# A hybrid encoder step on one core: the last two turns of the down projection as plain block products, the output stored in two parts, and the last h pair split inside its operand tiles

## The chip, the core and the metric

The kernel runs on one core of a Trainium2 chip. The time is that of one execution on the device, in microseconds (us); of several runs the median counts. The engines are TensorE (PE, with its weight loads shown as PEld), VectorE (DVE), ScalarE (ACT), GpSimd (POOL) and SyncE (SP), which here only issues DMAs. Each engine runs its own instructions in order and waits on semaphores for the others; ACT and POOL issue DMAs of their own as well.

## The reference, cut to what matters

One layer on 512 prompt frames (with 16 meta tokens ahead of them) and 64 sample frames: RMSNorm, a joint input projection, a pooling mixer and a differential attention, an output projection, and then the part that the change touches, a SwiGLU block and the last RMSNorm:

```python
D_MODEL, D_FF = 2048, 5632

def _rmsnorm(x, g, eps=EPS):
    xf = x.astype(jnp.float32)
    y = xf * lax.rsqrt(jnp.mean(xf * xf, axis=-1, keepdims=True) + eps)
    return (y * g.astype(jnp.float32)).astype(x.dtype)

def _swiglu(h, g_ffn, w_gate, w_up, w_down):
    n = _rmsnorm(h, g_ffn)
    return h + (jax.nn.silu(n @ w_gate) * (n @ w_up)) @ w_down

    y_prompt = _rmsnorm(h_p[:, N_META:], g_final)
    y_sample = _rmsnorm(h_s, g_final)
```

Everything is float32. The 512 + 64 = 576 tokens behind the block are handled together; the outputs are 512 and 64 rows of 2048.

## The kernel before

**Number format.** Each float32 operand of a product is split into a high part (a copy into TensorE's reduced format, on ACT) and a low part (the difference, on DVE). A product is three matmuls: high x high, high x low, low x high (L808 to L810). Tokens lie in the free dimension, in two halves of TN = 288.

**Seven products for eight.** The class `Seven` multiplies a weight block (2 x 2 blocks of 128) with an operand (2 feature rows x 2 token halves) by a scheme of seven block products. `prep` forms the sums and differences of weight blocks on DVE (L793 to L797) and splits the seven weight operands; `product` runs their matmuls for all feature pairs of the turn; `evac` adds the results in PSUM to the output.

**The down projection.** Its operand h, 5632 features by 576 tokens, is held in DRAM as 22 feature pairs `hd[0]` to `hd[21]`, each already combined into the seven operands of the scheme. In the numbering of these operands, index 0 is feature row 0 with token half 0, 3 is row 1 with half 0, 5 is row 1 with half 1, and 2 is the difference of the two halves of row 0. Pairs 0 to 20 are stored split (high and low); pair 21, the last made, is stored unsplit. A pair comes into SBUF as three tiles of two operands (`hc`, q = 0, 1, 2) and one half tile (`hh`, q = 3).

The work is 40 turns: five rounds over eight row pairs m of the output (256 output features each), each turn with up to five h pairs. The staggered `starts` give turns 32 to 39, the last round, 5, 5, 4, 4, 3, 3, 2 and 2 h pairs. A full turn is 7 x 5 x 3 = 105 matmuls, one of the last two 7 x 2 x 3 = 42. Turns alternate between the PSUM pools `mm` and `pj`. Row pair m of the output is added up in SBUF as `yt[m]`, four blocks of 288 tokens. Some of the sums go by an accumulating DMA from POOL: the shared first product in round 3 (L1106) and, for m under 6, two pieces of the last round by way of the buffers `ev` (L1101, L1102).

**Order.** The program is written in the order of the products, with `prep` three products ahead; `hooks` runs after each product. It loads an h pair when its first use is at most two turns off and a tile is free, behind the weight loads of the next turn on SP's queue. Pair 21 is read in seven pieces through two `ev` buffers, each then split into its `hc` tile by ACT (L1005) and DVE (L1006).

**The end.** `rows_out(m)` turns row pair m back into token rows: transposes on PE by 128 x 128 (L1136), the sum of squares on ACT (L1139), the product with the gain on DVE (L1142, L1146) into `yo`. It runs in the turn after the one that finishes the row pair. There are five token tiles (0 to 3 of 128 rows, 4 of 64). After the last row pair all five get their scale 1/rms at once (L1175 to L1182), and then `yo` is scaled and stored in 18 pieces of 256 KB (L1190 to L1194).

Of the kernel before, what the change touches and what calls it, by code (L numbers as in the profile page):

```python
# [50 lines left out]
def hymba_step(  # L51
# [945 lines left out]
    def h_operand(f, q):  # L997
        w, t = 2 if q < 3 else 1, h_slot(f, q)
        if f < NFP - 1:
            nc.sync.dma_start(out=t.bitcast(F32), in_=hd[f][:, 2 * q:2 * q + w])  # L1000
            return
        for i in range(w):
            s = dw.tile([P, TN], F32, name="ev", tag="ev", bufs=2)
            nc.sync.dma_start(out=s, in_=hd[f][:, 2 * q + i, 0])
            nc.scalar.activation(t[:, i, 0], s, AF.Copy)  # L1005
# [110 lines left out]
    def rows_out(m):  # L1116
# [5 lines left out]
        if m % 2 == 0:  # L1122
            for t in (0, 2):
                yo[t, m // 2] = full_slot([P, 1152], "yo", dtype=F32)[:, :1024].rearrange("p (t c) -> p t c", t=2)
        if m % 4 == 0:
            yo[4, m // 4] = full_slot([P, 1152], "yo", dtype=F32)[:, :1024]
        st, c0 = stat, m * 2 * P
        g = gfin[m // 4][:, c0 % 1024:c0 % 1024 + 256]
        for t in (0, 2, 4):
            nt = 2 if t < 4 else 1  # L1130
            rows = TT[t][1]
            pt = pz.tile([P, 512], F32, name="mm", tag="mm").rearrange("p (t c) -> p t c", t=2)[:rows, :nt]
            for u in range(nt):
                for i in range(2):
                    t0 = TT[t + u][0]
                    nc.tensor.transpose(out=pt[:, u, i * P:i * P + P], in_=hrow(2 * m + i)[:, t0:t0 + rows], identity=ident)  # L1136
            for u in range(nt):
                jk = dw.tile([P, 256], F32, name="jk", tag="jk", bufs=2)[:rows]
                nc.scalar.activation(jk, pt[:, u], AF.Square, accum_out=st[:rows, t + u, m:m + 1])  # L1139
# [93 lines left out]
```

## Time and profile before

| | us |
|---|---|
| median of 3 runs | 2314.15 |
| lowest, highest | 2313.45, 2318.22 |
| the profiled execution | 2311.8 |
| its span | 2310.0 |
| TensorE busy in it | 2252.7 |
| turn 31 starts | 2177.48 |
| turn 38 starts | 2270.35 |
| last transposes start | 2287.81 |
| first store issued | 2293.09 |

The span is the time from the first to the last event of the profiled execution; the execution's own time is 1.8 us longer. A row of a timeline has the start, the duration, the engine, the line, the operation and the names of output and inputs; in brackets is the idle time of the engine ahead of it and what ended it. Matmuls overlap in a pipeline, so the pitch from start to start is what one costs, not its duration.

### The profile page before, as it was taken

The page shows a single profiled execution, that of the slowest core. Times are in us where ns is not written, and L with a number is a line of the kernel's source. Part 1 is how long each engine was busy: PE and PEld are TensorE (multiplying, and loading weights), DVE is VectorE, ACT ScalarE, POOL GpSimd, SP SyncE. Part 2 cuts the span into 40 slices and gives each one's busy share as a digit, 9 for nine tenths or more (in the row PEclk, how much of TensorE's full clock was granted, in tenths as well). Part 3 has the DMA queues.
Part 4 walks back from the last instruction along what each step waited for, and adds up shares of the span by engine and source line. Part 5 has one row for each costly group of instructions (what it writes and reads, how often), then busy time and mean ns, then how long its engine had stood idle before and what let it go on. Part 6 is the DMA issues. An engine that isn't in the chain of part 4 may idle for free.

```text
span 2310.0 us, 43435 instructions
## 1 busy us (share of the span) xinstructions
PE 2252.7 (98%) x16815; PEld 2230.6 (97%) x16815; DVE 1904.8 (82%) x3496; ACT 1113.4 (48%) x2305; POOL 499.9 (22%) x452
## 2 busy tenths in 40 slices
PE   7999999999999899999999999999999999999995
PEld 6999999999999899999999999999999999999995
DVE  6888888875477889998999999999897788888787
ACT  5666666643244544444444444444444533333354
POOL 1100001000234223333343343333333000000110
PEclk9999999999999999999999999999999999999998
DMA  6433333323324244454444444435446778766844
GB/s 171 115 93 97 97 89 102 86 66 92 85 65 139 81 139 143 128 154 146 136 137 154 137 135 150 149 122 159 150 128 226 226 221 222 212 200 187 225 98 117
DMA packets 427362, 322.28 MB, mean 140 GB/s; under 512 B 13107, under 2 KB 397421, under 8 KB 427156
## 3 DMA queue, kind: packets, MB, share of 16 engines
q1 hardware_dynamic: 403616, 248.17, 36.7%
q0 software_dynamic: 22704, 69.90, 11.0%
q8 instruction: 132, 2.16, 0.4%
q10 hardware_dynamic: 836, 1.43, 0.2%
q14 instruction: 74, 0.61, 0.1%
HBM read 255.33 MB, written 62.03 MB: 137 GB/s over the span
## 4 chain that ended last, share of the span: by engine, by line
PE 89%; issue 5%; DVE 3%; DMA 1%; POOL 1%; ACT 1%; SPq 0%; POOLq 0%; DVEq 0%; ACTq 0%
PE mm L808 10%; PE pj L808 10%; PE pj L810 10%; PE mm L810 10%; PE pj L809 10%; PE mm L809 10%; PE pj L112 6%; PE pj L114 6%; PE pj L113 6%; PE mm L114 3%; PE mm L112 3%; PE mm L113 3%; PE S L426 1%; PE S L425 1%; PE T L454 1%
## 5 line engine op out<-in xcount | busy, mean ns | idle before, releaser
L838 DVE TENSOR_TENSOR ws<-raw,ws 128x512 fp32r<-128x512 f32 x430 | 393.9, 951 | 57.1 <-ACT ws L837 56.9
L837 ACT ACTIVATE ws<-raw 128x512 fp32r<-128x512 f32 x430 | 264.0, 629 | 360.6 <-DVE raw L795 121.1
L808 PE MATMUL mm<-xc,ws 128*128 128x288 f32 x1232 | 365.4, 297 | 7.6 <-ACT ws L837 7.4
L808 PE MATMUL pj<-xc,ws 128*128 128x288 f32 x1232 | 365.1, 296 | 3.1 <-ACT ws L837 3.1
L809 PE MATMUL mm<-xc,ws 128*128 128x288 f32 x1232 | 363.4, 295 | 0.0
L809 PE MATMUL pj<-xc,ws 128*128 128x288 f32 x1232 | 363.2, 295 | 0.0
L810 PE MATMUL pj<-xc,ws 128*128 128x288 f32 x1232 | 361.8, 294 | 0.8 <-DVE ws L838 0.8
L810 PE MATMUL mm<-xc,ws 128*128 128x288 f32 x1232 | 361.7, 294 | 0.2 <-DVE ws L838 0.2
L112 PE MATMUL pj<-x,ws 128*128 128x296 f32 (+1 forms) x1024 | 317.9, 311 | 9.6 <-DMA lv<-in_lambda_q_dram 5.2
L113 PE MATMUL pj<-x,ws 128*128 128x296 f32 (+1 forms) x1024 | 307.2, 300 | 0.0
L114 PE MATMUL pj<-x,ws 128*128 128x296 f32 (+1 forms) x1024 | 305.7, 299 | 0.0
L808 PEld LDWEIGHTS mm<-xc,ws 128*128 128x128 f32 x1232 | 232.0, 188 | 8.4 <-ACT ws L837 8.0
L808 PEld LDWEIGHTS pj<-xc,ws 128*128 128x128 f32 x1232 | 232.0, 188 | 3.3 <-ACT ws L837 3.3
L810 PEld LDWEIGHTS pj<-xc,ws 128*128 128x128 f32 x1232 | 233.2, 189 | 1.1 <-DVE ws L838 1.1
L810 PEld LDWEIGHTS mm<-xc,ws 128*128 128x128 f32 x1232 | 233.3, 189 | 0.4 <-DVE ws L838 0.4
L809 PEld LDWEIGHTS mm<-xc,ws 128*128 128x128 f32 x1232 | 233.0, 189 | 0.1
L809 PEld LDWEIGHTS pj<-xc,ws 128*128 128x128 f32 x1232 | 232.9, 189 | 0.0
L137 ACT ACTIVATE ws<-wraw,vcols 128x128 fp32r<-128x128 f32 x512 | 169.4, 392 | 106.9 <-PE pj L114 87.9
L1082 ACT ACTIVATE ws<-raw 128x640 fp32r<-128x640 f32 (+3 forms) x190 | 130.5, 688 | 184.1 <-PE mm L810 68.4
L112 PEld LDWEIGHTS pj<-x,ws 128*128 128x128 f32 x1024 | 193.2, 189 | 14.7 <-ACT x L106 9.6
L113 PEld LDWEIGHTS pj<-x,ws 128*128 128x128 f32 x1024 | 194.2, 190 | 0.4
L114 PEld LDWEIGHTS pj<-x,ws 128*128 128x128 f32 x1024 | 193.1, 189 | 0.0
(369 smaller groups left out, 5738.3 us busy)
## 6 DMA issues: line engine op xcount, KB each, us to landing
raw<-in_w_up_dram SPq DMA_DIRECT2D x88, 512.0 KB, 3.8
raw<-in_w_gate_dram SPq DMA_DIRECT2D x84, 512.0 KB, 5.0
hc<-hd SPq DMA_DIRECT2D x63, 576.0 KB, 6.0
raw<-in_w_down_dram SPq DMA_DIRECT2D x112, 320.0 KB, 7.1
wraw<-in_w_in_dram SPq DMA_DIRECT2D x64, 512.0 KB, 4.1
wraw<-in_w_out_dram SPq DMA_DIRECT2D x32, 512.0 KB, 4.0
hd<-hi POOLq DMA_DIRECT2D x21, 576.0 KB, 3.5
hd<-ho POOLq DMA_DIRECT2D x21, 576.0 KB, 4.2
```

What stands on the lines that cost most here:

```text
L112: nc.tensor.matmul(ps, lhsT=w(0), rhs=x(0), start=first, stop=False)
L113: nc.tensor.matmul(ps, lhsT=w(0), rhs=x(1), start=False, stop=False)
L114: return nc.tensor.matmul(ps, lhsT=w(1), rhs=x(0), start=False, stop=last)
L137: nc.scalar.activation(ws[:, 0, k, :], r[:, k, :], AF.Copy, scale=g)
L425: nc.tensor.matmul(ps, lhsT=self.q[:, m, qs], rhs=kt[:, m, c0:c1], start=True, stop=False)
L426: nc.tensor.matmul(ps, lhsT=self.q[:, 2 + m, qs], rhs=kt[:, m, c0:c1], start=False, stop=True)
L808: nc.tensor.matmul(ps, lhsT=w(0), rhs=x(0), start=first and j == 0, stop=False, skip_group_check=True)
L809: nc.tensor.matmul(ps, lhsT=w(0), rhs=x(1), start=False, stop=False, skip_group_check=True)
L810: mm = nc.tensor.matmul(ps, lhsT=w(1), rhs=x(0), start=False, stop=j == self.nj - 1, skip_group_check=True)
L837: nc.scalar.activation(ws[:, 0], src[:, k:k + WK], AF.Copy)
L838: nc.vector.tensor_tensor(ws[:, 1], src[:, k:k + WK], ws.bitcast(F32)[:, 0], op=ALU.subtract)
L1082: nc.scalar.activation(ws[:, 0], src, AF.Copy)
```

## The change

The code shown here is the part that decides; the arithmetic of the scale is rearranged too (a reciprocal and four short DVE operations in place of a reciprocal and five), and `rows_out` takes a list of token tiles, of 128-column blocks and of the column for its sum of squares.

```diff
+    PLAIN = 2
...
         if f < NFP - 1:
             nc.sync.dma_start(out=t.bitcast(F32), in_=hd[f][:, 2 * q:2 * q + w])
             return
-        for i in range(w):
-            s = dw.tile([P, TN], F32, name="ev", tag="ev", bufs=2)
-            nc.sync.dma_start(out=s, in_=hd[f][:, 2 * q + i, 0])
-            nc.scalar.activation(t[:, i, 0], s, AF.Copy)
-            nc.vector.tensor_tensor(t[:, i, 1], s, t.bitcast(F32)[:, i, 0], op=ALU.subtract)
+        nc.sync.dma_start(out=t.bitcast(F32)[:, :, 1], in_=hd[f][:, 2 * q:2 * q + w, 0])
+        whole.append((7 * now[0][0] + now[0][1] + 4, t))
+
+    def h_split(t):
+        f = t.bitcast(F32)
+        tc.keep_in_program_order(nc.scalar.activation(t[:, :, 0], f[:, :, 1], AF.Copy))
+        tc.keep_in_program_order(nc.vector.tensor_tensor(t[:, :, 1], f[:, :, 1], f[:, :, 0], op=ALU.subtract))
...
-        if queue and i in (0, 2, 4, 6) and first_use[queue[0][0]] <= n + 2 and h_free(*queue[0], n, i):
+        if whole and whole[0][0] <= 7 * n + i:
+            h_split(whole.pop(0)[1])
+        if queue and i in (0, 2, 4, 6) and first_use[queue[0][0]] <= n + 2 + queue[0][0] // 20 and h_free(*queue[0], n, i):
...
+        if n == len(turns) - PLAIN - 2 and i == 6:
+            plain_load()
+        if n == len(turns) - PLAIN - 1 and i >= 3:
+            plain_split(i - 3)
...
+    def plain_sum(ps, m, i, terms, start):
+        ops = [(pw[m, two], j, hc[f, q][:, b]) for two, q, b in terms for j, f in enumerate(pf)]
...
+    def plain_turns():
+        now[0] = (len(turns) - PLAIN, 0)
+        cols_ = [(m, i) for m in plain for i in range(2)]
+        b = {}
+        for m, i in cols_:
+            b[m, i] = pz.tile([P, 512], F32, name="mm", tag="mm")[:, :TN]
+            plain_sum(b[m, i], m, i, ((0, 0, 0),), True)
+            y_add(m, 2 * i + 1, b[m, i])
+        for k, (m, i) in enumerate(cols_):
+            plain_sum(b[m, i], m, i, ((1, 1, 1),), False)
+            y_add(m, 2 * i, b[m, i])
+            if k == 0:
+                rows_out(plain[0] - 1)
+        for k, (m, i) in enumerate(cols_):
+            ps = pj.tile([P, 512], F32, name="pj")[:, :TN]
+            plain_sum(ps, m, i, ((0, 1, 0), (1, 2, 1)), True)
+            y_add(m, 2 * i + 1, ps)
+            if k < 2:
+                rows_out(plain[k], (0,))
+            if k == 1:
+                row_scale(0, 2, 8)
+                for c in range(4):
+                    store_part(0, c, c % 2 == 1)
+            if k == 2:
+                rows_out(plain[0], (2, 4))
+        rows_out(plain[1], (2, 4), (0,))
+        rows_out(plain[1], (2, 4), (1,), 8)
+        for c in range(2):
+            store_part(1, c)
+        row_scale(2, 5, 9, ((1, 2), (1, 3, True)))
...
-    for n, (m, j0, j1) in enumerate(turns):
+    for n, (m, j0, j1) in enumerate(turns[:-PLAIN]):
...
     run(down, hooks, done=7 * EARLY, order=ORDER)
-    rows_out(NR - 1)
...
+    plain_turns()
```

Turns 38 and 39 (row pairs 6 and 7 with h pairs 20 and 21) no longer use the seven products. Per 128 output features there are now four block products, from operands 0, 3, 2 and 5 of the h pair. The first, row 0 with token half 0, is a part of both halves' results: it is added to the second half's output and stays in PSUM, where the product of row 1 with half 0 completes the first half. The second half then gets row 0 with operand 2 and row 1 with operand 5. That is 8 block products of 2 x 3 matmuls a turn, 48 where 42 were. All four output column blocks get token half 0 first, then half 1. Token tiles 0 and 1 lie in half 0; their scale and stores are written among the products of half 1, those of tiles 2 to 4 behind them.

The h pairs 20 and 21 may be loaded one turn earlier than before, and pair 21 comes as whole tiles into the place of its low part; ACT then writes the high part beside it and DVE the low part in place, four products behind the load.

On SP's queue, from the half tile of pair 19 on (`hd_9881`; `hd_9882` is pair 20 and `hd_9883` pair 21; `raw` is a weight piece of the turn after next, of which a turn has four; `ev` the two buffers). Before:

```order
L786 DMA raw<-in_w_down_dram 128x5x128 x3
L1000 DMA hh<-hd_9881 128x576
L786 DMA raw<-in_w_down_dram 128x5x128 x5
L1000 DMA hc_25228<-hd_9882 128x1152
L1000 DMA hc_25269<-hd_9882 128x1152
L1000 DMA hc_25309<-hd_9882 128x1152
L786 DMA raw<-in_w_down_dram 128x5x128 x3
L1000 DMA hh<-hd_9882 128x576
L786 DMA raw<-in_w_down_dram 128x5x128
L1004 DMA ev<-hd_9883 128x288 x2
L786 DMA raw<-in_w_down_dram 128x5x128 x2
L1004 DMA ev<-hd_9883 128x288 x2
```

The same stretch of SP's queue in the changed kernel:

```order
L786 DMA raw<-in_w_down_dram 128x5x128 x3
L1002 DMA hh<-hd_9881 128x576
L786 DMA raw<-in_w_down_dram 128x5x128
L1002 DMA hc_25078<-hd_9882 128x1152
L1002 DMA hc_25119<-hd_9882 128x1152
L1002 DMA hc_25159<-hd_9882 128x1152
L786 DMA raw<-in_w_down_dram 128x5x128 x3
L1002 DMA hh<-hd_9882 128x576
L786 DMA raw<-in_w_down_dram 128x5x128
L1004 DMA hc_25236<-hd_9883 128x2x288
L1004 DMA hc_25277<-hd_9883 128x2x288
L1004 DMA hc_25319<-hd_9883 128x2x288
```

Both pairs moved ahead of four weight pieces, one turn; pair 21 takes three tile loads (and a half one behind two more pieces) where seven pieces went through `ev`.

On ACT, the splits of pair 21 among the weight splits (`ws`) of turns 31 and 32. Before:

```order
L1005 ACTIVATE hc_25386<-ev 128x288
L1082 ACTIVATE ws<-wt 128x640
L1005 ACTIVATE hc_25386<-ev 128x288
L1082 ACTIVATE ws<-raw 128x640
L1005 ACTIVATE hc_25434<-ev 128x288
L1082 ACTIVATE ws<-raw 128x640
L1005 ACTIVATE hc_25434<-ev 128x288
L1005 ACTIVATE hc_25481<-ev 128x288
```

The same on ACT in the changed kernel, where the place is one turn earlier:

```order
L1009 ACTIVATE hc_25236<-hc_25236 128x2x288
L1092 ACTIVATE ws<-raw 128x640
L1092 ACTIVATE ws<-wt 128x640
L1009 ACTIVATE hc_25277<-hc_25277 128x2x288
L1092 ACTIVATE ws<-raw 128x640 x2
L1009 ACTIVATE hc_25319<-hc_25319 128x2x288
```

One split now stands where two stood, with two weight splits between one and the next.

On DVE, the end of the program (`ones_v` holds the sums and scales, `y_20862` and `y_20863` are row pairs 6 and 7). Before, everything from the first scaling on comes last, in one run:

```order
L1104 TENSOR_TENSOR y_20863<-pj,y_20863 128x288
L1142 TENSOR_TENSOR yo<-mm,gfin 128x2x256 x2
L1146 TENSOR_TENSOR yo<-mm,gfin 64x256
L1175 TENSOR_REDUCE ones_v<-ones_v 128x5
L1177 RECIPROCAL ones_v<-ones_v 128x5
L1178 TENSOR_SCALAR ones_v<-ones_v 128x5
L1179 TENSOR_TENSOR ones_v<-ones_v 128x5
L1180 TENSOR_TENSOR ones_v<-ones_v 128x5
L1181 TENSOR_SCALAR ones_v<-ones_v 128x5
L1182 TENSOR_TENSOR ones_v<-ones_v 128x5
L1190 TENSOR_SCALAR yo<-yo,ones_v 128x512 x12
L1190 TENSOR_SCALAR yo<-yo,ones_v 64x1024
```

In the changed kernel the first half's reduction (128x2) stands behind the second column of half 1:

```order
L1219 TENSOR_TENSOR y_20862<-pj,y_20862 128x288
L1151 TENSOR_TENSOR yo<-mm,gfin 128x2x256
L1159 TENSOR_REDUCE ones_v<-ones_v 128x2
L1219 TENSOR_TENSOR y_20863<-pj,y_20863 128x288
L1161 TENSOR_SCALAR ones_v<-ones_v 128x2
L1164 RECIPROCAL ones_v<-ones_v 128x2
L1165 TENSOR_TENSOR ones_v<-ones_v 128x2
L1166 TENSOR_TENSOR ones_v<-ones_v 128x2
L1167 SCALAR_TENSOR_TENSOR ones_v<-ones_v 128x2
L1177 TENSOR_SCALAR yo<-yo,ones_v 128x512 x2
L1151 TENSOR_TENSOR yo<-mm,gfin 128x2x256
L1219 TENSOR_TENSOR y_20863<-pj,y_20863 128x288
```

Two scalings of token tile 0 now stand ahead of the last sum into `y_20863` (ACT has two more); between the reduction and its scale stands the sum of the third column, which waits for PE.

More of the change, by code (lines that the diff above doesn't have):

```diff
@@ L1114, in hymba_step, with rows_out @@
     TT = [(t0, min(P, NQ - t0)) for t0 in range(0, NQ, P)]
-    def rows_out(m):
+    def rows_out(m, tiles=(0, 2, 4), blks=(0, 1), into=None):
         if not gfin:
@@ L1121, in rows_out @@
                 gfin.append(g)
[L1122 to L1129, printed above, removed]
+        into, c0, w = m if into is None else into, (m * 2 + blks[0]) * P, len(blks) * P
+        g = gfin[m // 4][:, c0 % 1024:c0 % 1024 + w]
+        for t in tiles:
             nt = 2 if t < 4 else 1
+            part = (t, m // 2 if nt == 2 else m // 4)
+            if part not in yo:
+                o = full_slot([P, 1152], "yo", dtype=F32)[:, :1024]
+                yo[part] = o.rearrange("p (t c) -> p t c", t=2) if nt == 2 else o
             rows = TT[t][1]
@@ L1153, in finished, with plain_load @@
             rows_out(turns[n - 1][0])
+    plain = [m for m, j0, j1 in turns[-PLAIN:]]
+    pf = range(*turns[-1][1:])
+    assert all(turns[-1 - k][1:] == turns[-1][1:] for k in range(PLAIN)) and len(pf) == 2
+    praw, pw = {}, {}
+    def plain_load():
+        src = w_down[0].rearrange("(j two p) n -> p two j n", p=P, two=2)
+        for two in range(2):
+            for m in plain:
+                a = rw.tile([P, DJ, P], F32, name="raw", tag="raw", bufs=7).rearrange("p a b -> p (a b)")
+                praw[m, two] = a = a[:, :512].rearrange("p (j n) -> p j n", j=2)
+                nc.sync.dma_start(out=a, in_=src[:, two, pf[0]:pf[-1] + 1, m * 256:m * 256 + 256])
@@ new lines, in plain_split @@
+    def plain_split(k):
+        m, two = plain[k % 2], k // 2
+        ws = dw.tile([P, 2, DJ, P], F32R, name="ws", tag="ws", bufs=4).rearrange("p i a b -> p i (a b)")
+        pw[m, two] = ws = ws[:, :, :512].rearrange("p i (j n) -> p i j n", j=2)
+        nc.scalar.activation(ws[:, 0], praw[m, two], AF.Copy)
+        nc.vector.tensor_tensor(ws[:, 1], praw[m, two], ws.bitcast(F32)[:, 0], op=ALU.subtract)
+    def plain_sum(ps, m, i, terms, start):
+        ops = [(pw[m, two], j, hc[f, q][:, b]) for two, q, b in terms for j, f in enumerate(pf)]
+        for k, (w, j, x) in enumerate(ops):
+            cs = slice(i * P, i * P + P)
+            nc.tensor.matmul(ps, lhsT=w[:, 0, j, cs], rhs=x[:, 0], start=start and k == 0, stop=False, skip_group_check=True)
+            nc.tensor.matmul(ps, lhsT=w[:, 0, j, cs], rhs=x[:, 1], start=False, stop=False, skip_group_check=True)
+            nc.tensor.matmul(ps, lhsT=w[:, 1, j, cs], rhs=x[:, 0], start=False, stop=k == len(ops) - 1, skip_group_check=True)
@@ new lines, in y_add @@
+    def y_add(m, blk, ps):
+        y = yt[m][:, blk]
+        nc.vector.tensor_tensor(y, ps, y, op=ALU.add)
+    def plain_turns():
[28 more added lines that the diff above has]
+        row_scale(2, 5, 9, ((1, 2), (1, 3, True)))
+        for t in (2, 3):
+            for c in range(4):
+                store_part(t, c, c == 3, nc.scalar if c == 3 else nc.sync)
+        for c in range(2):
+            store_part(4, c, c == 1, nc.scalar if c == 1 else nc.sync)
```

57 lines of the change are left out of this document (30 added, 27 removed).

## The prediction

> **What bounds the kernel now.** First the page's span, its table of engines and the chain that ended last:
>
> ```profile
> span 2310.0 us, 43435 instructions
> PE 2252.7 (98%) x16815; PEld 2230.6 (97%) x16815; DVE 1904.8 (82%) x3496; ACT 1113.4 (48%) x2305; POOL 499.9 (22%) x452
> PE 89%; issue 5%; DVE 3%; DMA 1%; POOL 1%; ACT 1%; SPq 0%; POOLq 0%; DVEq 0%; ACTq 0%
> ```
>
> TensorE is the bound: 57 us of 2310 without a matmul. The change touches only the last 160 us, so next I read the busy time of the engines there, turn by turn (a turn of the down projection is one row pair with up to five h pairs, 105 matmuls at most), with turns 21 and 23 (counted from 0) for comparison. Columns: stretch, length, busy us of PE, its weight loads, VectorE, ScalarE, GpSimd (instructions), granted clock, DMA share, GB/s.
>
> ```profile
> 2038.60:2052.50 13.90, 13.90 (x108) 13.90 (x107) 11.59 (x19) 5.19 (x8) 0.00 (x0) 1.00 0.34 96
> ...
> 2066.40:2080.30 13.90, 13.90 (x107) 13.90 (x106) 11.59 (x19) 5.17 (x7) 0.00 (x0) 1.00 0.77 244
> ...
> 2135.90:2149.80 13.90, 13.90 (x108) 13.90 (x107) 11.62 (x19) 5.18 (x7) 1.27 (x1) 1.00 0.90 245
> 2149.80:2163.70 13.90, 13.90 (x107) 13.90 (x106) 11.62 (x19) 5.18 (x7) 1.26 (x1) 1.00 0.65 159
> 2177.70:2189.50 11.80, 11.80 (x90) 11.70 (x88) 6.87 (x12) 3.51 (x6) 2.43 (x3) 1.00 0.99 272
> 2189.50:2193.00 3.50, 0.13 (x2) 0.00 (x0) 0.89 (x3) 1.36 (x3) 0.00 (x0) 0.89 0.63 179
> 2193.00:2198.60 5.60, 5.50 (x21) 5.08 (x22) 5.45 (x10) 3.00 (x7) 0.00 (x0) 0.50 0.27 79
> ```
>
> A full turn takes 13.9 us with PE never idle. Turn 31 does not: PE stands from 2189.5 to 2193.0, and then has its clock halved. Its timeline, with what ended the wait, and the ScalarE and SP rows behind it:
>
> ```profile
> 2177.48 0.29 PE L808 MATMUL pj<-hc,ws 128*128 128x288 f32 x1
> 2189.34 0.29 PE L810 MATMUL pj<-hc,ws 128*128 128x288 f32 x1
> 2193.09 0.58 PE L808 MATMUL pj<-hh,ws 128*128 128x288 f32 x1 [3.46 <-ACT hc L1005]
> 2199.18 0.29 PE L810 MATMUL mm<-hc,ws 128*128 128x288 f32 x1
> 2191.64 0.44 ACT L1005 ACTIVATE hc<-ev 128x288 fp32r<-128x288 f32 x1 [5.98 <-DMA ev<-hd]
> 2184.59 1.70 SPq L1004 DMA_DIRECT2D ev<-hd  x2
> ```
>
> This is h pair 21, read through two `ev` buffers: two pieces at a time, each pair of loads held until the last pieces have been split. ScalarE sat 5.98 us at the head of its queue for a piece issued at about 2185, and the weight splits queued behind it kept PE waiting.
>
> The end is the second place: no PE work, 4.72 MB of output going out at the DMA's rate.
>
> ```profile
> 2285.87 0.30 PE L810 MATMUL pj<-hh,ws 128*128 128x288 f32 x1
> 2287.81 0.88 PE L1136 MATMUL mm<-ident,y 128*128 128x128 f32 x6 [0.81 <-DVE y L1104]
> 2292.58 5.50 DVE L1190 TENSOR_SCALAR yo<-yo,ones_v 128x512 f32<-128x512 f32 x13
> 2293.09 11.86 SPq L1191 DMA_DIRECT2D out_dram<-yo  x13
> 2295.00:2298.00 3.00, 0.00 (x0) 0.00 (x0) 3.00 (x8) 1.86 (x3) 0.00 (x0) 0.50 1.04 376
> 2306.00:2307.00 1.00, 0.00 (x0) 0.00 (x0) 0.00 (x0) 0.00 (x0) 0.00 (x0) 0.50 1.06 295
> 2307.00:2308.00 1.00, 0.00 (x0) 0.00 (x0) 0.00 (x0) 0.00 (x0) 0.00 (x0) 0.50 0.31 86
> ```
>
> The last product starts at 2285.87, the first scaling at 2292.58, the bytes run out after 2307, and the span ends at 2310.0: 24.1 us from the last product to the end, 17.4 of them from the first scaling on.
>
> **Part 1, h pair 21 split in its own tiles.** From its first matmul at 2177.48 (turn 31) to the ninth matmul of turn 32 at 2199.18 the PE starts 113 matmuls later in 21.70 us. At the pitch of the same turn before the wait, (2189.34 - 2177.48) / 89 = 0.133 us, these take 15.0. The wait and the slow clock behind it cost **6.7 us**: about 3.6 of standing, 3.1 of half clock.
>
> After the change pair 20 is loaded in turn 29 instead of 30 and pair 21 in turn 30 instead of 31, in three whole tiles and a half one, and each split stands four products behind its load, about 8 us. When whole-tile loads leave SP now (turns 22, 23, 24 and 30), and what one takes to land:
>
> ```profile
> 2053.54 1.36 SPq L1000 DMA_DIRECT2D hc<-hd  x3
> ...
> 2067.48 1.36 SPq L1000 DMA_DIRECT2D hc<-hd  x3
> ...
> 2081.41 1.36 SPq L1000 DMA_DIRECT2D hc<-hd  x3
> ...
> 2164.80 1.36 SPq L1000 DMA_DIRECT2D hc<-hd  x3
> ...
> hc<-hd SPq DMA_DIRECT2D x6, 576.0 KB, 6.2
> ```
>
> Pair 21 now leaves in that place, 2164.8 to 2166.2, with half the bytes a tile, and lands 6.2 us later, 2171.0 to 2172.4. Its first split comes on ScalarE behind the first weight split of turn 31, which runs about when the fourth product of turn 30 is done, some 2172. So the wait should vanish, or be under 1 us at a place where ScalarE is some three products (6 us) ahead of PE. First use is in turn 32, at about 2191, a turn later. The splits themselves get fewer: 4 + 4 instead of 7 + 7 instructions on ScalarE and VectorE, out of turn 31's last third into turns 30 and 31, where the windows show VectorE busy 11.6 of 13.9 us. I cost them at nothing: PE's 13.9 us cover them.
>
> What the earlier loads may cost is DMA room. A turn without h loads has a share of 0.34, with them 0.77 (turns 21 and 23 above), so a whole pair takes 0.43 x 13.9 = 6.0 us. From turn 25 on every turn also adds one partial row sum by DMA: turns 28 and 29 (0.90 and 0.65, one pair) are 21.5 us together, so a turn's own traffic is (21.5 - 6.0) / 2 = 7.8 us. Turns 28, 29, 30, 31 then hold 13.8, 13.8, about 10.8 and 7.8 plus the gain vector (now under the 0.99), where each has 13.9. Turns 28 and 29 are full, not over. Turns 22 to 24 load whole pairs in a row now (the three SP rows) without a PE wait, though at 0.77. Bounds: nothing, to one new wait like the one seen, 6.7. I take nothing, being nearest to the row at 0.90, in which PE never idles. POOL's order stays; SP's is passed only by the h loads, each ahead of one turn's weight pieces, which that estimate holds.
>
> The granted clock is 0.50 after a wait of 3.6 us and 1.00 again some 6 us later. The Trainium skill (TensorE: Matmul & The Clock Gate, "What's actually happening") says the clock halves only after an idle window of about 3.4 us. The trace agrees with the halving. By that rule a left-over wait of 2 us would cost 2.0; by the trace's ratio (6.7 for 3.6) it would cost 3.7.
>
> **Part 2, the last two turns.** Time zero is the first matmul of turn 38:
>
> ```profile
> 2270.35 0.30 PE L808 MATMUL mm<-hc,ws 128*128 128x288 f32 x1
> 2268.07 1.25 PE L1136 MATMUL mm<-ident,y 128*128 128x128 f32 x10
> 2269.08 0.38 PE L808 MATMUL pj<-hh,ws 128*128 128x288 f32 x1
> 2274.95 0.66 PE L1136 MATMUL mm<-ident,y 128*128 128x128 f32 x4 [1.11 <-DMA y<-ev]
> ```
>
> Now 84 matmuls and 20 transposes bring the last product to +15.5 (2285.87). After: 2 turns x 8 products x 2 h pairs x 3 = 96 matmuls, 12.8 us; 24 transposes (10 of row pair 5, 4 + 4 of the first two token tiles, 6 of row pair 6) at 0.101 us (ten in 2269.08 - 2268.07) = 2.4; six changes back to products at 0.09 (the first matmul behind transposes lasts 0.38 in place of 0.29) = 0.6; the wait for row pair 5's DMA sum, which lands at 2274.95 while PE arrives at +30 x 0.133 = 2274.3, 0.6. Last product at **+16.4, 0.9 later**. The weight splits shrink from 14 + 14 to 4 + 4 and the eight weight combinations go, off the path but for the 1.11 us of PE waiting that now stands there; four weight loads of 256 KB replace eight of 128, behind the same SP rows.
>
> The first half of the tokens: its second row pair is transposed at 12.8 x 72/96 + 18 x 0.101 + 0.6 + 0.4 = +12.4. Two squares, the sum and the scale follow. The costs by operation, in this part of the trace:
>
> ```profile
> L1139 ACT ACTIVATE jk<-mm 128x256 f32<-128x256 f32 x32 | 11.7, 379 | 6.3 <-PE mm L1136 6.3
> L1104 DVE TENSOR_TENSOR y<-mm,y 128x288 f32<-128x288 f32 x20 | 9.0, 451 | 0.5 <-PE mm L810 0.5
> L1142 DVE TENSOR_TENSOR yo<-mm,gfin 128x512 f32<-128x512 f32 x16 | 10.7, 686 | 2.2 <-ACT jk L1139 2.0
> L1190 DVE TENSOR_SCALAR yo<-yo,ones_v 128x512 f32<-128x512 f32 x12 | 4.8, 480 | 0.0
> L1193 ACT ACTIVATE yo<-yo,ones_v 128x512 f32<-128x512 f32 x4 | 2.7, 715 | 1.5 <-DVE ones_v L1182 1.1 <-ACT yo L1193 0.5
> 2290.99 0.18 DVE L1175 TENSOR_REDUCE ones_v<-ones_v 128x5 f32<-128x40 f32 x1
> ```
>
> The scale takes 2292.58 - 2290.99 = 1.6 us now. In VectorE's order the third column's sum into y stands between the reduction and the rest, so the scale waits for that product, done near +14; with 0.45 for the sum and about 0.9 for the rest the first scaling is at **+15.3**, the first store at +15.8 by the 0.5 between 2292.58 and 2293.09. Four stores of 256 KB leave there, under PE's last product. Nothing else uses the DMA then.
>
> The second half: last product +16.4, its sum +17.2, three transposes +17.7. ScalarE meanwhile has two scalings of the first half (1.4) and six squares in its queue, and reaches the last three squares at about +17.9, done +18.8. VectorE follows with the last product with the gain (+19.2), two scalings of token tile 1 (+20.1), the reduction (+20.3), the root on ScalarE, one more scaling (0.5) and four short operations: first scaling of the second half at **+22.0**. Now it is at +22.2 (2292.58). So the chain is no shorter; what is gained is bytes. Eight of the eighteen stores, 2.10 MB, have left before; at 376 GB/s that is **5.6 us**. Four of these eight go only between +20 and +22 and take till about +23.7, 0.6 us into the others' time. So from +22.0 the end is 17.4 - 5.6 + 0.6 = 12.4 later, +34.4, against 39.65 now: **5.2 us gained**. Bounds: all eight hidden and ScalarE's queue short, 8; the halves not overlapping at all, with PE's 0.9 and the second scale of 1.6 on the path, a loss of 2.5.
>
> Sum against the profiled execution: 6.7 + 5.2 = **12 us**, span 2310.0 to 2298. That execution took 2311.8, 2.3 under the median 2314.15 of the runs shown; taken from the median, **2302**. A measurement tells about 0.2%, 4.6 us, from no change.
>
> **Rivals.** (a) The wait for pair 21 stays in part: its loads land late in full queues (one took nearly 6 us to be waited for now). 2 to 4 of the 6.7 us remain: 2305. For it: the 0.99. Against: it leaves a turn earlier. (b) The change doesn't do what it says at the end: scaling and stores of the first half, held in VectorE's in-order queue behind later sums, leave with the rest. Then the tail loses 0 to 2.5 and only the 6.7 remain: about 2309. Against: the program order puts the scale right behind the third column's sum. (c) Slower: turns 28 to 30 run the DMA at 13.8 of 13.9 us a turn, and backlog grows from turn to turn until weight pieces come late. It decides when the pieces lag by more than the lead of their splits, some three products, 6 us. Each late turn then has the wait and the half clock now seen, 6.7. One: 2314.15 - 12 + 6.7 = 2309; two: 2315.6; all of turns 29, 30 and 31: 2322. For it: 0.90 already; against: the sum does not exceed a turn.
>
> **How the numbers follow.** Forecast 73%; (a) 10%; (b) 7%, half of it over the 4.6 us; (c) one late turn 4%, likewise counted mostly faster, two 3%, three 3%. Faster by over 0.2%: 0.73 + 0.10 + 0.04 + 0.03 = 0.90; within: 0.07; slower 0.03. The range goes from 2297 (tail at its bound of 8, and 2 of run spread) to 2309, (b) and one late turn.
>
> **What would show it.** Part 1: no row of PE with a wait on ScalarE's h split, granted clock 1.00 through turn 31, turn 32 starting 13.9 us after turn 31; wrong if PE waits for weight splits in turns 29 to 31. Part 2: stores issued while PE still multiplies, last product 16 to 17 us after the first plain one, first scaling of the second half 5 to 6 us behind it, and some 12 from there to the end; wrong if no store leaves before the last product, or if the DMA idles between the two parts for long.

## The result and the profile after

| | us |
|---|---|
| kernel before, median of 6 runs (lowest, highest) | 2314.22 (2313.03, 2318.22) |
| changed kernel, median of 6 runs (lowest, highest) | 2299.16 (2296.99, 2300.69) |
| ratio, 95% interval | 0.9933, 0.9921 to 0.9946 |

The changed kernel is faster by 15.1 us; 12 were forecast, and 2297 to 2309 was the range. The page of its profile, in the order in which that of before was read:

```profile
span 2297.1 us, 43416 instructions
PE 2249.1 (98%) x16827; PEld 2227.9 (97%) x16827; DVE 1897.9 (83%) x3479; ACT 1112.4 (48%) x2300; POOL 500.9 (22%) x452
PE 93%; DVE 2%; issue 2%; DMA 1%; ACT 0%; POOL 0%; DVEq 0%; POOLq 0%; ACTq 0%
```

The time without a matmul fell from 57.3 to 48.0 us and TensorE's busy time from 2252.7 to 2249.1, in which matmuls at half clock count as busy: 9.3 of the 12.9 us by which the span is shorter are standing. The shares of the last chain don't measure this: "issue" from 5% to 2% of some 2300 us would be some 70. Turns 28 to 32 by the same stretches of 13.9 us (columns as in the prediction; each stretch starts within half a us of its turn):

```profile
2136.80:2150.70 13.90, 13.90 (x107) 13.90 (x107) 11.63 (x19) 5.18 (x7) 1.27 (x1) 1.00 0.90 242
2150.70:2164.60 13.90, 13.90 (x107) 13.90 (x106) 11.62 (x19) 5.19 (x8) 1.26 (x1) 1.00 1.00 277
2164.60:2178.40 13.80, 13.80 (x106) 13.80 (x105) 11.99 (x20) 6.32 (x9) 1.27 (x1) 1.00 0.91 236
2178.40:2192.30 13.90, 13.90 (x106) 13.90 (x106) 12.52 (x21) 6.08 (x9) 2.44 (x3) 1.00 0.82 203
2192.40:2206.30 13.90, 13.90 (x107) 13.90 (x106) 11.80 (x19) 5.59 (x8) 2.21 (x2) 1.00 0.56 124
```

TensorE is busy for all of every turn at a granted clock of 1.00; turn 31 is now like any other. The DMA share of turn 29 is 1.00, and TensorE waits for nothing there. The starts of turns 30, 31 and 38 on TensorE's timeline, and the end:

```profile
2164.34 0.30 PE L808 MATMUL mm<-hc,ws 128*128 128x288 f32 x1
2178.36 0.29 PE L808 MATMUL pj<-hc,ws 128*128 128x288 f32 x1
2264.55 0.30 PE L1213 MATMUL mm<-hc,ws 128*128 128x288 f32 x1
2279.92 0.30 PE L1215 MATMUL pj<-hc,ws 128*128 128x288 f32 x1
2281.35 0.52 PE L1145 MATMUL mm<-ident,y 128*128 128x128 f32 x3 [0.81 <-ACT jk L1148]
2279.36 0.88 DVE L1177 TENSOR_SCALAR yo<-yo,ones_v 128x512 f32<-128x512 f32 x2
2279.88 12.95 SPq L1180 DMA_DIRECT2D out_dram<-yo  x15
2283.06 0.86 DVE L1177 TENSOR_SCALAR yo<-yo,ones_v 128x512 f32<-128x512 f32 x2
2285.66 3.12 DVE L1177 TENSOR_SCALAR yo<-yo,ones_v 128x512 f32<-128x512 f32 x7
```

From turn 31 to turn 38 it is 2264.55 - 2178.36 = 86.19 us where it was 2270.35 - 2177.48 = 92.87: 6.68 gained. From turn 38 to the end of the span it is 32.55 us where it was 39.65: 7.1 gained. SP's row of stores starts at 2279.88, 0.04 us before the last matmul of the last product starts. Its bytes move behind that product (the DMA share is the second number from the right):

```profile
2279.00:2280.00 1.00, 1.00 (x10) 1.00 (x9) 0.93 (x4) 0.99 (x4) 0.00 (x0) 1.00 0.00 0
2280.00:2281.00 1.00, 0.55 (x5) 0.28 (x3) 1.00 (x3) 1.00 (x5) 0.00 (x0) 1.00 0.28 100
2281.00:2282.00 1.00, 0.52 (x3) 0.28 (x3) 0.94 (x4) 0.96 (x8) 0.00 (x0) 1.00 0.99 375
```

So the first half's stores run under the second half's row work, and not under the last product. The two gains sum to 13.8; the spans differ by 12.9, since turn 31 came 0.9 us later in this execution for reasons ahead of the change, and the medians by 15.1.

### The profile page after: what moved, and what is told of

It reads as the page before. It is cut to its first block, busy times and chain, and to the rows that moved or that the text cites. A ratio compares the mean times of both kernels' runs of the same rounds, so it can differ in the third digit from the quotient of the medians.

```text
span 2297.1 us, 43416 instructions
## 1 busy us (share of the span) xinstructions
PE 2249.1 (98%) x16827; PEld 2227.9 (97%) x16827; DVE 1897.9 (83%) x3479; ACT 1112.4 (48%) x2300; POOL 500.9 (22%) x452
## 2 busy tenths in 40 slices
DMA packets 426226, 322.28 MB, mean 140 GB/s; under 512 B 12995, under 2 KB 396285, under 8 KB 426020
## 4 chain that ended last, share of the span: by engine, by line
PE 93%; DVE 2%; issue 2%; DMA 1%; ACT 0%; POOL 0%; DVEq 0%; POOLq 0%; ACTq 0%
PE pj L808 10%; PE pj L810 10%; PE mm L808 10%; PE pj L809 10%; PE mm L810 10%; PE mm L809 10%; PE pj L112 6%; PE pj L114 6%; PE pj L113 6%; PE mm L114 3%; PE mm L112 3%; PE mm L113 3%; PE S L426 1%; PE S L425 1%; PE T L454 1%
## 5 line engine op out<-in xcount | busy, mean ns | idle before, releaser
L1092 ACT ACTIVATE ws<-raw 128x640 fp32r<-128x640 f32 (+2 forms) x180 | 126.5, 703 | 186.0 <-PE mm L810 67.4
```

The lines of the kernel that those rows point to most:

```text
L1092: nc.scalar.activation(ws[:, 0], src, AF.Copy)
```

## The experiments

All of them are read by two stretches, since both lie behind the place where the kernels begin to differ in their waits: from turn 30 to turn 38 (part 1), and from turn 38 to the end of the span (part 2). Each start is the row of the first matmul of the turn on TensorE's timeline:

| kernel | turn 30 | turn 38 | 30 to 38 | 38 to the end | time, us | ratio to before |
|---|---|---|---|---|---|---|
| before | 2163.46 | 2270.35 | 106.89 | 39.65 | 2314.22 | 1 |
| changed | 2164.34 | 2264.55 | **100.21** | **32.55** | 2299.16 | 0.9933 (0.9921 to 0.9946) |
| e1, part 1 alone | 2169.55 | 2269.76 | 100.21 | 39.14 | 2306.0 | 0.9969 (0.9959 to 0.9979) |
| e2, part 2 alone | 2161.50 | 2268.79 | 107.29 | 32.21 | 2306.25 | 0.9973 (0.9961 to 0.9984) |
| e3, earlier load only | 2164.84 | 2269.29 | 104.45 | 40.11 | 2311.15, one run | |
| e4, split in place only | 2162.80 | 2263.01 | 100.21 | 38.99 | 2303.76, one run | |
| e0, changed again | 2165.24 | 2265.45 | 100.21 | 32.45 | 2301.07 | 0.9945 (0.9930 to 0.9959) |
| e5, one scale | 2164.16 | 2264.38 | 100.22 | 36.22 | 2303.56 | 0.9957 (0.9942 to 0.9973) |
| e6, first half sooner | 2164.74 | 2264.96 | 100.22 | 31.64 | 2298.85 | 0.9938 (0.9925 to 0.9951) |
| e8, load in turn 31 | 2163.43 | 2263.64 | 100.21 | 32.46 | 2298.16 | 0.9931 (0.9918 to 0.9945) |
| e7, one extra copy | 2163.29 | 2263.56 | 100.27 | 32.24 | 2297.82, one run | |
| e7, two extra copies | 2167.51 | 2268.57 | 101.06 | 32.63 | 2302.99, one run | |

The time of the kernel before is that of the first group of runs; in the groups of the other kernels it was 2313.43 (e1 to e4), 2313.78 (e0, e5, e6, the first e7) and 2313.93 (e8, the second e7), and each ratio is to that of its own group.

The first column is a warning. In twelve profiled executions turn 30 starts anywhere from 2161.50 to 2169.55, though nothing is changed ahead of turn 29. A single time holds this spread of 8 us; the stretch from 30 to 38 is the same to 0.01 us in seven executions of six kernels. For part 1 the table is a better witness than a single time. The last stretch repeats less well. The old end took 38.99 to 40.11 us in four executions (before, e1, e3, e4), the new one 32.21 to 32.63 in six (changed, e0, e2, e8 and both e7), so part 2 is worth 6.4 to 7.9. The spread lies in the stores: from the last product to the first scaling of the last stores the four took 6.70 to 6.71, the six 5.72 to 5.74.

The changed kernel ran once more in the second group of runs, as the standard for e5 and e6 (e0; the kernel before took 2313.78 there):

> The changed kernel again, unchanged, as the standard of this group of runs, for the two kernels that are made from it. Expected: 2299 us, ratio to the kernel before 0.993.

It took 2301.07, 1.9 more than in the first group; the two intervals overlap, and its stretches are the same to 0.1 us.

### Each part alone

Part 1 alone is the kernel before with three of the diff's changes (the load, the split and the earlier condition); part 2 alone is the changed kernel with these put back:

```diff
-        nc.sync.dma_start(out=t.bitcast(F32)[:, :, 1], in_=hd[f][:, 2 * q:2 * q + w, 0])
-        whole.append((7 * now[0][0] + now[0][1] + 4, t))
+        for i in range(w):
+            s = dw.tile([P, TN], F32, name="ev", tag="ev", bufs=2)
+            nc.sync.dma_start(out=s, in_=hd[f][:, 2 * q + i, 0])
...
-        if whole and whole[0][0] <= 7 * n + i:
-            h_split(whole.pop(0)[1])
-        if queue and i in (0, 2, 4, 6) and first_use[queue[0][0]] <= n + 2 + queue[0][0] // 20 and h_free(*queue[0], n, i):
+        if queue and i in (0, 2, 4, 6) and first_use[queue[0][0]] <= n + 2 and h_free(*queue[0], n, i):
```

> Part 1 alone: pairs 20 and 21 loaded a turn earlier, pair 21 split in its tiles; the last two turns and the stores as before. My theory: the two parts stand in different places and add. Turn 31 then lasts 13.9 us instead of 19.4 with no PE wait, and from the start of turn 31 to the start of turn 38 pass 86.2 us as in the changed kernel (92.9 before): 6.7 us faster than before, ratio 0.9971. Rival: part of the saved wait comes back later, because the last two turns as before need their weights and sums at the pace of the old schedule: under 4 us faster.

> Part 2 alone: plain products and stores in two parts, h pairs 20 and 21 loaded and split as before. My theory: the wait of 3.5 us and the half clock in turn 31 are there again, and from the first matmul of turn 38 to the end pass 32.5 us instead of 39.65: 7.1 us faster than before, ratio 0.9969, and both parts together about 13.8. Rival: part 2 gains only because nothing of the queue behind pair 21 is left: under 4 us faster.

Both came out near these expectations: part 1 gains 6.68 us from turn 30 to 38, and part 2 takes 32.21 from turn 38 to the end. The product of the two ratios, 0.9969 x 0.9973 = 0.9942, lies in the interval of the whole: as far as the intervals tell, the parts add. In the trace of part 2 alone the old wait stands where it stood. TensorE's row, and the ScalarE row behind it:

```profile
2192.16 0.37 PE L808 MATMUL pj<-hh,ws 128*128 128x288 f32 x1 [3.33 <-ACT hc L1006]
2190.72 0.44 ACT L1006 ACTIVATE hc<-ev 128x288 fp32r<-128x288 f32 x1 [5.65 <-DMA ev<-hd]
```

### What in part 1 took the wait away

The prediction gave two reasons at once: pair 21 leaves a turn earlier, and it is split as whole tiles without the two buffers. e3 has the first alone, e4 the second alone. The two edits, in this order, each against the kernel before:

```diff
-        if queue and i in (0, 2, 4, 6) and first_use[queue[0][0]] <= n + 2 and h_free(*queue[0], n, i):
+        if queue and i in (0, 2, 4, 6) and first_use[queue[0][0]] <= n + 2 + queue[0][0] // 20 and h_free(*queue[0], n, i):
```

```diff
-        for i in range(w):
-            s = dw.tile([P, TN], F32, name="ev", tag="ev", bufs=2)
...
+        nc.sync.dma_start(out=t.bitcast(F32)[:, :, 1], in_=hd[f][:, 2 * q:2 * q + w, 0])
+        whole.append((7 * now[0][0] + now[0][1] + 4, t))
...
+        if whole and whole[0][0] <= 7 * n + i:
+            h_split(whole.pop(0)[1])
```

> Of part 1 only the earlier load: pairs 20 and 21 may be loaded three turns ahead of their use, but pair 21 still goes in seven pieces through two buffers, each split right behind its load. Theory A (it is the two buffers: ScalarE waits at the head of its queue for each piece's landing, about 5 to 6 us, wherever that stands): the PE wait moves to turn 30 and stays 2 to 4 us, with half clock behind it, time within 3 us of before. Theory B (it is the load being late): no PE wait, about 6.7 us faster.

> Of part 1 only the whole tiles split in place, four products behind their load, with the loads in turn 31 as before. Theory A (the two buffers and splits right behind the load made the wait): no PE wait or one under 1 us, about 6 us faster. Theory B (the load is late): the loads leave at 2179 and later beside the gain vector in a stretch with a DMA share of 0.99, land 6 to 9 us later, and the splits of the last tiles reach PE late: a PE wait of 1 to 4 us at the start of turn 32, with half clock behind it if it is over some 3 us.

With the earlier load and the two buffers, the wait moves a turn ahead with the load and only shrinks. ScalarE's timeline of e3, and TensorE's:

```profile
2170.34 0.45 ACT L1005 ACTIVATE hc<-ev 128x288 fp32r<-128x288 f32 x1 [2.53 <-DMA ev<-hd]
2175.85 0.45 ACT L1005 ACTIVATE hc<-ev 128x288 fp32r<-128x288 f32 x1 [3.48 <-DMA ev<-hd]
2178.87 0.45 ACT L1005 ACTIVATE hc<-ev 128x288 fp32r<-128x288 f32 x1 [1.61 <-DMA ev<-hd]
2180.21 0.74 ACT L1082 ACTIVATE ws<-raw 128x640 fp32r<-128x640 f32 x1 [0.90 <-DVE raw L795]
...
2177.30 0.37 PE L808 MATMUL mm<-hh,ws 128*128 128x288 f32 x1 [0.31 <-ACT hc L1005]
2181.00 0.40 PE L808 MATMUL pj<-hc,ws 128*128 128x288 f32 x1 [1.47 <-ACT ws L1082]
2181.86 0.61 PE L810 MATMUL pj<-hc,ws 128*128 128x288 f32 x1 [0.33 <-DVE ws L1083]
```

ScalarE stands three times at the head of its queue for a piece in `ev`; a weight split that TensorE needs at 2181 runs at 2180.21 behind them. What ended its last wait is VectorE's weight sum (L795), which stands in VectorE's queue behind the low-part splits of the same pieces. The load was a turn earlier and its data were late again, because a piece may leave only when a buffer is free, and that waits for the split of the piece before. The kernel before shows this tie. VectorE's split, which frees a buffer, ends at 2184.56 and SP issues the next two pieces at 2184.59 (SP's row is in the prediction):

```profile
2184.10 0.46 DVE L1006 TENSOR_TENSOR hc<-ev,hc 128x288 fp32r<-128x288 f32 x1 [1.96 <-ACT hc L1005]
```

e4 loads when the kernel before did, and its splits stand four products behind the load. ScalarE's first one, and the window that holds turn 31 (2176.82 to 2190.83 there):

```profile
2185.67 0.67 ACT L1008 ACTIVATE hc<-hc 128x576 fp32r<-128x576 f32 x1
```

```profile
2177.00:2191.00 14.00, 14.00 (x107) 14.00 (x107) 12.19 (x20) 6.33 (x9) 2.43 (x3) 1.00 0.99 274
```

No idle time stands ahead of the split, and TensorE is busy throughout. The split in place is the whole of part 1's gain. It does two things at once, and no run separates them: the two buffers go, and the split stands four products behind its load instead of right behind it, where ScalarE waited for the landing. The earlier load was then taken out of the full change too, by the one line of e3 in reverse:

> The changed kernel with the load of the last column pair back in the turn in which the kernel before had it (one turn later than in the changed kernel); the split in the operand tiles and the plain products stay. Theory A (what held TensorE up was the two-buffer staging; the place of the load adds nothing): no wait for h in turns 30 to 32, 2299 to 2301 us, 0.993 to 0.9945 of the kernel before. Rival B (the later load comes too late beside the weights that the full change loads): a wait of 1.5 to 4 us for h in turn 31 or 32 with half the clock behind it, 2303 to 2307 us, 0.995 to 0.997.

Its stretch is again 100.21, its ratio 0.9931. The share of the DMA by turns 29 to 31 (each stretch starts 1 us behind its turn) shows what the earlier load does, and that it does no more:

```profile
2150.70:2164.60 13.90, 13.90 (x107) 13.90 (x106) 11.62 (x19) 5.18 (x7) 1.26 (x1) 1.00 0.59 140
2164.60:2178.40 13.80, 13.80 (x106) 13.80 (x105) 11.41 (x18) 5.13 (x7) 1.27 (x1) 1.00 0.96 263
2178.40:2192.30 13.90, 13.90 (x107) 13.90 (x106) 12.09 (x20) 6.22 (x10) 2.43 (x3) 1.00 0.99 276
```

Three turns of 1.00, 0.91 and 0.82 become 0.59, 0.96 and 0.99: the loads of the two pairs come a turn later.

### How near the transfers are to being the bound

The third rival was a DMA that falls behind in turns 28 to 30. So bytes were added: copies from memory to memory of the size of the whole-tile loads, whose data nothing uses. One kernel has them behind pair 20's loads (the first part of this edit), the other behind pair 21's as well (both parts):

```diff
             nc.sync.dma_start(out=t.bitcast(F32), in_=hd[f][:, 2 * q:2 * q + w])
+            if f == 20 and q < 3:
+                x = dram.tile([P, 2, 2, TN], F32, name=f"spare{f}{q}")
+                nc.sync.dma_start(out=x, in_=hd[f][:, 2 * q:2 * q + w])
...
+        if q < 3:
+            x = dram.tile([P, 2, 2, TN], F32, name=f"spare{f}{q}")
+            nc.sync.dma_start(out=x, in_=hd[f - 1][:, 2 * q:2 * q + w])
```

> The changed kernel with an extra copy of the same bytes from memory to memory behind each of the three whole loads of pair 20: 0.88 MB more to read and as much to write in turn 29, which doubles the load's part there. The extra copies' data are used nowhere. It asks how near the transfers of turns 28 to 30 are to being the bound. Theory A (full but not over, with some 6 us of lead before TensorE needs the tile): TensorE waits nowhere, or under 1 us, on h in turns 29 to 32, and the time is within 1 us of the changed kernel's. Rival B (already at the brink: the third rival of the prediction): a wait of 3 to 6 us for h or the second half's operands, half the clock behind it, 2305 to 2310 us.

> The changed kernel with the extra copies of pair 20 and, behind each of pair 21's three whole loads, one more of the same size, whose data are used nowhere: 3.5 MB more to move over turns 29 and 30. With pair 20's copies alone TensorE waited nowhere before the end, and turn 30 took a part of the load. Theory A (full but not over, some 6 us of lead): three turns' transfers come to about 13.9 + 5 + 10.8 + 10 us of 27.8, some 12 us over by bytes at the rate of the rows, more than the lead: TensorE waits 3 to 8 us for h or for a second half's weights in turns 30 to 32, and the time is 2304 to 2312 us. Rival B (the extra copies cost the engines far less than their bytes, so that one pair's copies prove no lead): no wait over 1 us, time within 2 us of the changed kernel's.

With one set of copies (three of 576 KB) no wait on h or on a weight split is left in these turns, and the stretch is 100.27. With two sets the only wait is 0.33 us, in turn 32, and the stretch is 101.06, 0.85 longer. The windows of the second one, shifted by some 3 us against its turns, and the row of the wait:

```profile
2150.70:2164.60 13.90, 13.90 (x107) 13.90 (x106) 11.60 (x19) 5.22 (x8) 1.26 (x1) 1.00 1.02 285
2164.60:2178.40 13.80, 13.80 (x106) 13.80 (x105) 10.19 (x16) 4.92 (x7) 1.27 (x1) 1.00 1.12 331
2178.40:2192.30 13.90, 13.90 (x106) 13.90 (x105) 12.15 (x21) 7.12 (x11) 2.42 (x3) 1.00 1.03 302
2192.30:2206.20 13.90, 13.57 (x101) 13.17 (x100) 13.01 (x22) 4.95 (x7) 1.29 (x1) 1.00 0.87 220
```

```profile
2196.50 0.40 PE L810 MATMUL mm<-hc,ws 128*128 128x288 f32 x1 [0.33 <-DVE ws L1099]
```

The expectation of 3 to 8 us of waiting for two sets was wrong. It took the share of 1.00 as a ceiling, and charged 5 us for the first set and 10 for the second, though both are of one size: each raises the 322.28 MB that the profile counts by 1.77 (the 0.88 of the other expectation is half of that). The engines moved 331 GB/s at 1.12 where the changed kernel's turn 29 moved 277 at 1.00. By an estimate from these rows, the 3.5 MB took 10.7 us (at 331) and not 15; turns 30 to 32 had 1.2, 2.5 and 6.1 us to spare ((1 - share) x 13.9 in the changed kernel). That would leave some 7 us of backlog at the end of turn 31, near the lead of 6 us that the prediction took, and the wait is in turn 32. Copies are another kind of transfer than loads into SBUF, so this tells the room, and not what a third pair would cost.

### What part 2's gain is made of

e5 keeps the plain products and the order of the last two turns, and takes the overlap away: one scale, and all stores behind it.

```diff
...
-            if k == 1:
-                row_scale(0, 2, 8)
-                for c in range(4):
-                    store_part(0, c, c % 2 == 1)
...
-        for c in range(2):
-            store_part(1, c)
-        row_scale(2, 5, 9, ((1, 2), (1, 3, True)))
-        for t in (2, 3):
+        row_scale(0, 5, 9)
+        for t in range(4):
```

> The changed kernel with one scale for all four tiles and all 18 stores behind the last product: the plain products and the order of the last two turns stay, the overlap of the first half's stores with the last product goes. Theory A (the tail's gain is that about half of the output is under way before the last product ends): the stretch from the first plain product to the end grows from 32.6 us back to 37 to 40 us, the first store comes about 5 us after the last product instead of before it, the time is 2304 to 2307 us (ratio to the kernel before 0.9957 to 0.997), and what is left below 1 is the wait that went from turn 31. Rival B (the plain products win by themselves, by fewer operations at the end): the stretch stays at 32.6 to 34 us and the time at 2299 to 2301 us, ratio 0.993 to 0.994.

36.22 us from turn 38 to the end lies between the two theories: both are half right. Theory A's premise isn't so, since in the changed kernel no output had moved when the last matmul of the last product started, at 2279.92 (share 0.00 from 2279 to 2280 above). The last product, the first scaling and the stores of e5:

```profile
2279.76 0.29 PE L1216 MATMUL pj<-hc,ws 128*128 128x288 f32 x1
2283.90 5.50 DVE L1178 TENSOR_SCALAR yo<-yo,ones_v 128x512 f32<-128x512 f32 x13
2284.41 11.89 SPq L1181 DMA_DIRECT2D out_dram<-yo  x13
```

Set beside before and the changed kernel, where the "first scaling" is the one that the last stores wait for:

| | turn 38 to the last product | to the first scaling | to the end | sum |
|---|---|---|---|---|
| before | 15.52 | 6.71 | 17.42 | 39.65 |
| e5, one scale | 15.38 | 4.14 | 16.70 | 36.22 |
| changed | 15.37 | 5.74 | 11.44 | 32.55 |

The plain products alone, in their order, are worth 3.4 us by this table, of which 0.7 lies behind the first scaling, where the old end varies by 1.1 in four executions. They cost TensorE no time, and they leave less row work behind the last product: 6 transposes in place of 10, and the first scaling follows 4.14 us behind it and not 6.71. The rearranged arithmetic of the scale has little part in it: from the reduction to the first scaling it is 1.46 us for 1.59. The overlap is worth another 3.7: 5.3 less at the end, of which it gives 1.6 back. Two scalings on ScalarE hold up the squares, so that the last transposes start 1.43 us behind the last product instead of 0.98; two scalings of tile 1 (0.78) stand ahead of VectorE's reduction and one (0.39) ahead of the scale. By time the overlap is 2303.56 - 2301.07 = 2.5 us in the runs of this group, whose intervals overlap.

e6 tries to get this 1.6 back. It writes the first half's row work and scale one column of half 1 sooner, behind the first, stores tile 0 behind the second column and tile 1 behind the third, and leaves nothing between the last reduction and its scale:

```diff
-            if k < 2:
-                rows_out(plain[k], (0,))
-            if k == 1:
+            if k == 0:
+                rows_out(plain[0], (0,))
+                rows_out(plain[1], (0,))
                 row_scale(0, 2, 8)
+            if k in (1, 2):
                 for c in range(4):
-                    store_part(0, c, c % 2 == 1)
+                    store_part(k - 1, c, c % 2 == 1)
...
-        for c in range(2):
-            store_part(1, c)
-        row_scale(2, 5, 9, ((1, 2), (1, 3, True)))
+        row_scale(2, 5, 9)
```

> The changed kernel with the first half's last tiles put out one turn half sooner, tile 0 stored behind the second and tile 1 behind the third plain product, and nothing between the reduction and the scale of the second half. Theory A (the end is now set half by VectorE's queue behind the last product, half by the transfers): the three scalings of tile 1, which stand between the last product and the second half's reduction in the changed kernel (0.4 to 0.9 us each), leave that chain, the DMA engines are not half idle between the two parts, the second half's first scaling comes 1 to 2 us sooner and the end 1 to 2 us sooner: 2297 to 2298 us, 0.9993 to 0.9996 of the changed kernel. Rival B (the transfers of the whole output set the end, and the last of them starts when it did): under 0.5 us. Rival C (the earlier row work holds TensorE up in the last turn, since its operands aren't ready): TensorE's waits in the last turns grow from 0.8 us to over 2 us and the time is 1 to 3 us longer.

The second half's first scaling comes 0.7 us sooner behind the last product, 5.03 (2280.32 to 2285.35) for 5.74, where six executions of the changed end agree to 0.02; expected were 1 to 2. ScalarE's scalings of tile 1 now stand ahead of the squares, and the last transpose waits 0.94 us for VectorE. The stretch to the end is 31.64 for 32.55 (32.21 to 32.63 in the six), and the time 2298.85 against 2301.07, which the intervals don't tell apart. That it is faster by time is not shown. The windows of the changed kernel between its two parts of stores, and then those of e6:

```profile
2283.00:2284.00 1.00, 0.00 (x0) 0.00 (x0) 1.00 (x4) 0.00 (x0) 0.00 (x0) 1.00 0.57 215
2284.00:2285.00 1.00, 0.00 (x0) 0.00 (x0) 0.63 (x4) 0.91 (x2) 0.00 (x0) 0.66 0.63 238
2285.00:2286.00 1.00, 0.00 (x0) 0.00 (x0) 0.86 (x5) 0.35 (x1) 0.00 (x0) 0.50 0.97 361
...
2287.00:2288.00 1.00, 0.00 (x0) 0.00 (x0) 1.00 (x3) 0.55 (x1) 0.00 (x0) 0.50 1.04 381
```

```profile
2284.00:2285.00 1.00, 0.00 (x0) 0.00 (x0) 0.56 (x6) 0.30 (x1) 0.00 (x0) 0.81 1.03 395
2285.00:2286.00 1.00, 0.00 (x0) 0.00 (x0) 0.93 (x4) 0.65 (x2) 0.00 (x0) 0.50 0.49 188
2286.00:2287.00 1.00, 0.00 (x0) 0.00 (x0) 1.00 (x4) 0.68 (x2) 0.00 (x0) 0.50 0.30 111
```

The half-idle DMA between the two parts isn't filled, only moved: the first part ends sooner, and the second still waits for its scale. So the chain of row work behind the last product sets when the second part of the stores can start; from there to the end it is 11.4 us and 11.2.

## Why the prediction was right, step by step

**Part 1, 6.7 us, measured 6.68.** The size came from counting matmuls at the pitch of the same turn. That it holds to 0.02 is in part luck: in e2, with the same staging, the waits and their clock cost 107.29 - 100.21 = 7.08. The cause was named too broadly. "Pair 21 now leaves in that place" and "it leaves a turn earlier" were given as reasons, and e3, e4 and e8 show otherwise: alone, the earlier load took 2.4 of the 6.7, and with the split in place it adds nothing. The wait came from the staging, in which each load is tied to the split before it and each split stands right behind its load.

**DMA room, taken at nothing, and the third rival.** The estimate of 13.8 us for turn 29 stands against a measured share of 1.00, 13.9. Turn 30, put at 10.8, holds 12.6 by its share of 0.91, and turn 31, put at 7.8 and the gain vector, 11.4 by 0.82, both still under a turn. The rival of late turns was far from happening: with 1.77 MB of copies more TensorE waits nowhere in these turns, and with 3.5 MB it waits 0.33 us.

**The first rival**, a left-over wait, did not occur in the changed kernel, but it did in e3, with which its price can be compared. Its waits of 0.31 + 1.47 + 0.33 = 2.1 us cost 104.45 - 100.21 = 4.24. By the trace's ratio (6.7 for 3.6) they would be 3.9; the wait alone, 2.1, is too little. Most of the rest is the clock: 3.4 us at half, as the last section shows, are 1.7, together 3.8.

**Part 2, 5.2 us, measured 7.1.** The mechanism held in the main: the first half's bytes go early, and the second half's scaling sets when the rest can start. It did not hold that four stores run under the last product: their lead, forecast at 0.6 us, was 0.04, and it was the row work that hid them. Two terms were mis-sized by 1.0 us each. The last product was forecast at +16.4 and came at +15.37. Of that, 0.6 was the wait for row pair 5's sum: its transposes start at +4.0 and find it there,

```profile
2268.55 0.60 PE L1145 MATMUL mm<-ident,y 128*128 128x128 f32 x4
```

and 0.4 of the 0.6 that was charged for six changes between products and transposes was not paid. The stretch from the second half's first scaling to the end was forecast at 12.4 and is 11.44. That forecast started from 17.4, the one execution at hand; with the old end that stretch took 16.9 to 18.0 in four. So the record doesn't say whether this 1.0 is the 0.6 charged for tile 1's late stores, with the DMA half idle just then (0.57 and 0.63 above), or that spread. Between them, the forecast of 5.6 us from the last product to the scaling is 5.74. "The chain is no shorter; what is gained is bytes" holds for 6.0 of the 7.1 us; from turn 38 to that scaling the chain is 1.1 shorter (22.23 to 21.11). e5 shows what is under it: behind the last product the chain got 2.6 us shorter by the plain products, and the overlap gave 1.6 of these back.

**The second rival**, stores that leave with the rest, falls by the SP row at 2279.88, 5.8 us ahead of the second half's first scaling. e5 is near that case, with one scale and all stores behind it: 36.22 us, a gain of 3.4 in the tail where the rival gave it 0 to -2.5. The prediction did not see that the plain products gain without any overlap.

**The sum.** 6.68 + 7.1 = 13.8 in the traces, 15.1 by the medians; the difference lies within the intervals.

## What to carry to other kernels

A load that goes through two staging buffers, each piece split right behind its load, was late here even when it was written a turn earlier, since each piece waits for the split of the piece before; landing in the operand's own tile, with the split some products later, took the wait away. When the last output waits on a scale over all of its rows, look for an order that finishes a part of the rows in full before the last product: even without overlapped stores it shortened the row work behind that product here, by 2.6 us. And time a local change by the stretch between two marks in the trace, and see how well that stretch repeats: here turns 30 to 38 repeated to 0.01 us and the end with its stores to 0.4 or 1.1, where whole executions differ by several.

## What was not expected of the hardware

**Half the clock after less than 2 us of standing.** Windows of e3 from just before to just after its clock fell (granted clock in the third column from the right):

```profile
2178.40:2181.70 3.30, 1.66 (x11) 1.19 (x9) 3.15 (x6) 1.94 (x4) 0.00 (x0) 1.00 0.25 60
2181.70:2185.10 3.40, 3.25 (x13) 3.25 (x14) 3.40 (x7) 1.28 (x3) 1.26 (x1) 0.50 0.11 37
```

TensorE was busy for half of the first 3.3 us, and never stood for longer than 1.47; yet the clock fell to 0.50, for the 3.4 us after. In e1 a wait of 1.08 us near the end (TensorE's timeline, then the windows behind it) left the clock at 1.00:

```profile
2274.34 0.66 PE L1141 MATMUL mm<-ident,y 128*128 128x128 f32 x4 [1.08 <-DMA y<-ev]
```

```profile
2275.00:2276.00 1.00, 1.00 (x10) 1.00 (x9) 0.50 (x3) 0.77 (x4) 0.00 (x0) 1.00 0.00 0
2276.00:2277.00 1.00, 1.00 (x10) 1.00 (x9) 0.99 (x3) 0.00 (x0) 0.00 (x0) 1.00 0.00 0
2277.00:2278.00 1.00, 1.00 (x9) 0.76 (x7) 1.00 (x4) 0.99 (x5) 0.00 (x0) 1.00 0.00 0
```

The Trainium skill (TensorE: Matmul & The Clock Gate, "What's actually happening") has free-running windows of about 3.4 us and the clock halved after an idle one. The length agrees: 3.4 us at half in e3, and 6.8 in the kernel before, two windows (by shorter stretches of its trace, from about 2192.2 to 2199.1). That a window has to be idle does not: in e3 one with half of its time busy was enough. In the kernel before, too, the clock fell some 2.6 us into the wait: in the prediction's row from 2189.5 to 2193.0 the mean of 0.89 means about 0.8 us at half. Whether a single wait counts (1.08 left the clock alone, 1.47 did not) or what a window sums to (1.47 and 0.33 in e3), and how far it depends on where the wait falls, these runs don't show.

**A DMA share of 1.00 is not a ceiling.** It stood for 277 GB/s in turn 29 of the changed kernel, and 1.12 for 331 with the copies; the stores at the end of the changed kernel go at 361 to 381 at 0.97 to 1.04. What a share of 1.00 carries differs between these rows.
